# Column sums of squares on TensorE in place of VectorE adds, in the first two norms of a hybrid state-space backbone

## The chip, the cores and the metric

The kernel runs on one core of one Trainium2 chip. The metric is the device time of one execution in microseconds (us). The kernel before took 1124.67 us, the median of three runs (1123.05 to 1126.91).

## The reference

Two trunk layers work on 512 latent tokens of 1024 features, with a prefix of 256 context tokens. What matters here is the beginning of the first layer: a position embedding is added to x, then x and ctx are normalised by the root of the mean square over the features, scaled and shifted by a modulation that comes from `c` (for x) or `c_ctx` (for ctx), and projected.

```python
def rms_norm(x, g):
    xf = x.astype(jnp.float32)
    y = xf * lax.rsqrt(jnp.mean(xf * xf, axis=-1, keepdims=True) + EPS)
    return (y * g.astype(jnp.float32)).astype(x.dtype)
...
h = x + grid_pos_embed(ROWS, x.dtype)[None]
...
n_x = modulate(rms_norm(h, norm_mix_g[i]), sh1, sc1)
n_c = modulate(rms_norm(hc, norm_mix_g[i]), csh1, csc1)
```

Then come state-space groups (a scan over 512 + 256 tokens in 32 groups of 16 channels, with parameters that are discretised in the kernel), a convolution branch, an output projection, a squared-ReLU MLP, a second layer with a pooling mixer and another MLP, and a final norm.

## The kernel before, in words

Activations lie with features on the 128 partitions: x is `x0`, eight tiles `x0[:, d]` of 128 features by 512 tokens, ctx eight tiles of 128 by 256. A norm needs the sum of squares over all 1024 features of each token, that is, over eight tiles and over 128 partitions.

The program is written down as calls, and a planner lays the instructions of each engine in an order: it simulates the program with durations of its own, takes what is ready, and among that what was written first. Each engine then runs its queue strictly in that order, SyncE's queue of DMA issues too. So small work that is written later, such as the discretisation of the state-space parameters (`discretise`, L501, its tile is `scr`), stands between the steps of the norm on VectorE wherever the planner saw room, and a changed duration can move instructions in all queues of the program.

The opening is written in this order (L864 on): `u_load(d)` issues the DMAs of feature tile d (two blocks of modulation weights `wah` and `wraw`, a block of projection weights `wu`); `u_ada(d)` multiplies the modulation vectors with them (L363, 32 narrow matmul records on TensorE), ScalarE copies the result out of PSUM, a selector matmul folds it (L369), and VectorE finishes the tile `ab`. `norm_x` (L385) adds the position to each tile of x on VectorE, squares it on ScalarE, and adds the squares up on VectorE in two accumulators `sx`. `norm_c` (L397) does the same for ctx, two tiles at once, in one accumulator, with no position. Both end in `bcast_rsqrt` (L182): for each block of 128 tokens a matmul with the square as weights and one column of ones (L187) sums over the partitions and gives the tokens' sums as a column of 128 partitions; VectorE scales (`rs_x`, L122), GpSimd raises to the power -1/2 (`rs_y`), VectorE builds a diagonal (`dg`), a matmul with ones spreads it over all partitions (`ps_r`, L194), and ScalarE copies it to `Rs`.

Then `x_step(d)` (L460) scales a tile of x by `Rs` and modulation (`tn`), splits it into two reduced-precision parts (`nh`, `nl`), and multiplies it with the projection weights, twelve 512-wide matmuls into the four banks `ux` (L448 to L450). `c_step(d)` (L464) does it for ctx with six into `uc`; its order among the x steps is `CORD`. The weights are split into two parts by ScalarE and VectorE first (`w_step`, L452). When `discretise` is done, ScalarE writes its power tables `PG` and `PO` (L570). After the last tile, `ux` and `uc` are copied out and transposed (L904), and TensorE goes on with the convolution branch (`vgt`, L760) and the scan.

PSUM is full: bank tag `m` is one bank, used by `ps_ms` and then `ps_r` of each norm, `n` one bank for the modulation. Squares are held in tag `cv`, which has three buffers of 512 elements; two tiles of ctx squares fit one. ScalarE's copies and splits are L139, VectorE's additions L113, subtractions L116 and fused operations L125.

Of the kernel before, what the change touches and what calls it, by code (L numbers as in the profile page):

```python
# [8 lines left out]
F32 = mybir.dt.float32  # L9
F32R = mybir.dt.float32r  # L10
I32 = mybir.dt.int32
AF = mybir.ActivationFunctionType
# [4 lines left out]
D = 1024  # L17
L = 512
LC = 256
KT = 8  # L20
# [77 lines left out]
def body(tc, I, out, dbg=None):  # L98
    nc = tc.nc
    V, S, G, PE = nc.vector, nc.scalar, nc.gpsimd, nc.tensor  # L100
# [5 lines left out]
    def tt(e, o, a, b, op):  # L106
        e.tensor_tensor(o, a, b, op=op)

    def mul(e, o, a, b):
        e.tensor_tensor(o, a, b, op=OP.mult)  # L110

    def add(e, o, a, b):
        e.tensor_tensor(o, a, b, op=OP.add)  # L113
# [4 lines left out]
    def ts(o, a, s1, op0, s2=None, op1=None):  # L118
        if s2 is None:
            V.tensor_scalar(o, a, s1, None, op0=op0)  # L120
        else:
            V.tensor_scalar(o, a, s1, s2, op0=op0, op1=op1)  # L122
# [7 lines left out]
    def E(what, i):  # L130
        t = ENG[what]
        return {"V": V, "G": G, "S": S}[t[i % len(t)]]
# [4 lines left out]
    def copy(e, o, a):  # L137
        if e is S:
            S.activation(o, a, AF.Copy)  # L139
        else:  # L140
            e.tensor_copy(o, a)
# [10 lines left out]
    with tc.tile_pool(name="persist", bufs=1) as P, tc.tile_pool(name="ps", bufs=1, space=PSUM) as PS:  # L152
# [3 lines left out]
        ident = P.tile([128, 128], F32, name="ident")  # L156
        ones = P.tile([128, 128], F32, name="ones")
        mod = P.tile([128, 2, 6, KT], F32, name="mod")

        def smv(n):  # L160
            o, w = SM[n]
            return sm[:, o:o + w]
# [3 lines left out]
        cv = smv("cv").rearrange("p (s j) -> p s j", s=3)  # L166


        def rsqrt_small(ps_ap, m, n, scale):
            x = P.tile([128, 4], F32, name="rs_x", tag="rs_x", bufs=2)[:m, :n]  # L170
            y = P.tile([128, 4], F32, name="rs_y", tag="rs_y", bufs=2)[:m, :n]
            ts(x, ps_ap, scale, OP.mult, EPS, OP.add)
            tt(G, y, x, mhalf[:m, :n], OP.pow)
            return y

        def blocks(ntok):
            nj = -(-ntok // 128)
            while ntok % nj:
                nj += 1
            return nj, ntok // nj  # L180

        def bcast_rsqrt(sums, ntok, dim, tag="m"):  # L182
            nj, m = blocks(ntok)
            ps = bank("ps_ms", tag)
            for j in range(nj):
                for i, sq in enumerate(sums):
                    PE.matmul(ps[:m, j:j + 1], sq[:, j * m:(j + 1) * m], ones[:, 0:1], start=i == 0,  # L187
                              stop=i == len(sums) - 1)
            y = rsqrt_small(ps[:m, :nj], m, nj, 1.0 / dim)
            dg = tmp("dg")[:m, 0:ntok]  # L190
            mul(V, dg.rearrange("p (a b) -> p a b", a=nj), ident[:m, None, :m].to_broadcast([m, nj, m]),
                y[:, :, None].to_broadcast([m, nj, m]))
            pr = bank("ps_r", tag)
            PE.matmul(pr[:, :ntok], ones[:m], dg, start=True, stop=True)  # L194
            return pr[:, :ntok]
# [4 lines left out]
        def bank(nm, tag):  # L200
            return PS.tile([128, 512], F32, name=nm, tag=tag, bufs=dict(s=2, c=2, m=1, n=1)[tag])

        def tmp(nm, n=512, dt=F32):
            return P.tile([128, 512], dt, name=nm, tag="t", bufs=NTMP)[:, :n]

        def htile(nm, shape):
            return P.tile(shape, F32, name=nm, tag="H", bufs=1)
# [44 lines left out]
        def add_pos_k(e, t, d):  # L252
            hv = t[:, d].rearrange("p (k r m) -> p k r m", k=T, r=8)
            if d < 4:
                pe = posr[:, d, None, :, None]
            else:
                pe = posc[:, d - 4].rearrange("p (m k) -> p k m", k=T)[:, :, None, :]
            add(e, hv, hv, pe.to_broadcast([128, T, 8, 8]))
# [46 lines left out]
        def mixer0(P0):  # L305
# [16 lines left out]
            def w4(nm, tag, dt=F32, n=512):  # L322
                w = dict(cv=SLOT, g=1024, r=2 * GQ * NJ).get(tag, 512)
                return P0.tile([128, w], dt, name=nm, tag=tag, bufs=SLOTS[tag])[:, :n]
# [7 lines left out]
            x0 = htile("x0", [128, KT, L])  # L332
            load_x(x0, "xK")
            ctx = P0.tile([128, KT, LC], F32, name="ctx", tag="A")
# [42 lines left out]
            def small(n=NG, dt=F32):  # L377
                r = scr[:, used[0]:used[0] + n]
                used[0] += n
                return r.bitcast(dt) if dt is not F32 else r  # L380

            sx = P0.tile([128, 2, L], F32, name="sx", tag="ysb")
            Rs = [small(L), small(LC)]

            def norm_x():  # L385
                for d in range(KT):
                    add_pos_k(E("pos", d), x0, d)
                    if d < 2:
                        S.activation(sx[:, d], x0[:, d], AF.Square)
                    else:  # L390
                        q = w4("sq", "cv")
                        S.activation(q, x0[:, d], AF.Square)
                        add(V, sx[:, d % 2], sx[:, d % 2], q)
                add(V, sx[:, 0], sx[:, 0], sx[:, 1])
                copy(S, Rs[0], bcast_rsqrt([sx[:, 0]], L, D))

            def norm_c():  # L397
                qs = []
                for d in range(0, KT, 2):
                    q = w4("sq", "cv")  # L400
                    S.activation(q.rearrange("p (a b) -> p a b", a=2), ctx[:, d:d + 2], AF.Square)
                    if qs:
                        add(V, qs[0], qs[0], q)
                    qs.append(q)
                add(V, qs[0][:, 0:LC], qs[0][:, 0:LC], qs[0][:, LC:2 * LC])
                copy(S, Rs[1], bcast_rsqrt([qs[0][:, 0:LC]], LC, D))


            Br_, Bi_ = (P0.tile([128, NG * PH], F32, name="Bx", tag="K2", bufs=2) for _ in range(2))
# [454 lines left out]
            u_load(0)  # L864
            u_ada(0)
            norm_x()
            u_load(1)
            w_step(0)
            x_step(0)
            u_ada(1)  # L870
            norm_c()
            cf = None
            for d in range(1, KT):
# [27 lines left out]
            for i in range(0, NG, 4):  # L901
                ps = bank("ps_u", UT[i // 4])
# [72 lines left out]
        with tc.tile_pool(name="pre", bufs=1) as P0:  # L975
            EPOS = (V, G, V, G, V, G, V, G)
            h, oparts = mixer0(P0)


        with tc.tile_pool(name="main", bufs=1, reuse_waits="tile") as M:  # L980
# [5 lines left out]
            for t, tk in enumerate(HALF):  # L986
                for d in range(KT):
                    ps = tuple(p for p in (1, 0) if (p, t, d) in oparts)
# [156 lines left out]
            for tk in HALF:  # L1145
                n = tk.stop - tk.start
# [122 lines left out]
```

## Time and profile before

| | |
|---|---|
| median of three runs | 1124.67 us |
| profiled execution | 1127.26 us, its span 1125.1 us, around it 2.2 us |
| TensorE busy | 1045.0 us of the span, 7342 matmul records |
| VectorE busy | 810.7 us |
| ScalarE busy | 514.6 us |
| HBM traffic | 158 GB/s over the span |

Times in the rows are microseconds from the span's start, unless marked ns. PE is TensorE's matmul, PEld its weight load (which overlaps it), DVE is VectorE, ACT ScalarE, POOL GpSimd, SP SyncE. L187 is line 187 of the kernel. An fp32 matmul shows as two matmul records. Of several instructions that a row merges (x4), it gives the first start and their busy time together. A matmul's end is modelled, so a row of matmuls lasts somewhat into the next one.

### The profile page before, as it was taken

Reading aid. Unit: us, or ns where it says so; the run is one execution under the profiler, and the core shown is the slowest. Engines: PE = TensorE matmul, PEld = TensorE weight load, DVE = VectorE, ACT = ScalarE, POOL = GpSimd, SP = SyncE. Lnnn points to the kernel's source line nnn. Section 1 sums busy time; section 2 is a strip of 40 time slices with the busy share of each in tenths; the row PEclk is TensorE's granted clock in tenths of the full one; section 3 lists DMA queues with packets and bytes.
Section 4 is the critical chain, followed back from the end, with each engine's and each line's share of the span. In section 5 each row is a group of like instructions: output and inputs, shape, how many; then the busy total and the mean of one; then the engine's idle time right before and its main releaser. Section 6 shows DMA issues by size and latency. Waiting matters only on the chain.

```text
span 1125.1 us, 18913 instructions
## 1 busy us (share of the span) xinstructions
PE 1045.0 (93%) x7342; PEld 892.9 (79%) x7342; DVE 810.7 (72%) x1511; ACT 514.6 (46%) x910; POOL 23.8 (2%) x44
## 2 busy tenths in 40 slices
PE   3879998985998999999999999989989999999996
PEld 2657665544788988888789999989989988888896
DVE  7965699778688989868746679899866553343365
ACT  4365544454755643313325456566545332133253
POOL 0002000000000000000000000000000000000000
PEclk9999899997899999999999999999989999999998
DMA  9430634145546788878745555545535522233252
GB/s 348 146 128 30 184 85 148 44 123 187 160 137 208 208 281 290 304 230 282 242 149 170 182 174 186 162 133 177 160 121 181 178 94 94 95 108 97 94 169 94
DMA packets 63594, 185.09 MB, mean 165 GB/s; under 512 B 8464, under 2 KB 14608, under 8 KB 63376
## 3 DMA queue, kind: packets, MB, share of 16 engines
q1 hardware_dynamic: 63504, 183.87, 50.6%
q8 instruction: 58, 0.95, 0.3%
q14 instruction: 32, 0.26, 0.1%
HBM read 175.22 MB, written 2.10 MB: 158 GB/s over the span
## 4 chain that ended last, share of the span: by engine, by line
PE 53%; DMA 8%; DVE 6%; ACT 1%; issue 1%; POOLq 0%; POOL 0%; DVEq 0%; ACTq 0%
PE ps L150 17%; PE ps L149 17%; PE ps L148 17%; DMA wraw<-in_wadaT 5%; DMA wraw<-in_w 3%; DVE junk L1000 2%; DVE wlo L116 2%; ACT whi L139 1%; PE ps_o L148 0%; PE ps_r L194 0%; DVE tn L125 0%; PE ps_o L150 0%; PE ps_o L149 0%; PE ps_p L150 0%; PE ps_p L148 0%
## 5 line engine op out<-in xcount | busy, mean ns | idle before, releaser
L139 ACT ACTIVATE whi<-wraw 128x1024 fp32r<-128x1024 f32 (+1 forms) x232 | 231.7, 1000 | 397.2 <-PE ps L149 268.9
L116 DVE TENSOR_TENSOR wlo<-wraw,whi 128x1024 fp32r<-128x1024 f32 (+1 forms) x232 | 266.3, 1149 | 107.4 <-ACT whi L139 104.5
L148 PE MATMUL ps<-nh,whi 128*128 128x256 f32 (+3 forms) x768 | 245.8, 322 | 4.4 <-ACT nh L285 2.5
L150 PE MATMUL ps<-nh,wlo 128*128 128x256 f32 (+3 forms) x768 | 246.4, 322 | 1.8 <-DVE wlo L116 1.7
L149 PE MATMUL ps<-nl,whi 128*128 128x256 f32 (+3 forms) x768 | 246.7, 322 | 1.2 <-DVE nl L125 1.2
L148 PE MATMUL ps<-hh,whi 128*128 128x512 f32 (+3 forms) x768 | 244.3, 318 | 0.0
L150 PE MATMUL ps<-hh,wlo 128*128 128x512 f32 (+3 forms) x768 | 243.7, 317 | 0.1
L149 PE MATMUL ps<-hl,whi 128*128 128x512 f32 (+3 forms) x768 | 243.4, 317 | 0.0
L148 PEld LDWEIGHTS ps<-nh,whi 128*128 128x128 f32 x768 | 148.0, 194 | 15.7 <-ACT nh L285 3.7
L150 PEld LDWEIGHTS ps<-nh,wlo 128*128 128x128 f32 x768 | 148.0, 193 | 13.2 <-DVE wlo L116 3.1
L149 PEld LDWEIGHTS ps<-nl,whi 128*128 128x128 f32 x768 | 148.1, 193 | 11.8 <-DVE nl L125 1.7
L150 PEld LDWEIGHTS ps<-hh,wlo 128*128 128x128 f32 x768 | 144.2, 188 | 12.0 <-DVE wlo L116 0.9
L149 PEld LDWEIGHTS ps<-hl,whi 128*128 128x128 f32 x768 | 144.3, 188 | 10.6
L148 PEld LDWEIGHTS ps<-hh,whi 128*128 128x128 f32 x768 | 144.5, 188 | 9.9
L125 DVE SCALAR_TENSOR_TENSOR h<-ps,mod,h 128x512 f32<-128x512 f32 (+3 forms) x96 | 54.9, 571 | 85.9 <-PE ps L150 85.9
L1000 DVE SCALAR_TENSOR_TENSOR junk<-wraw,csil 128x1024 f32<-128x1024 f32 x56 | 68.3, 1220 | 19.9 <-DMA wraw<-in_wadaT 19.6
L116 DVE TENSOR_TENSOR hl<-rl,hh 128x256 fp32r<-128x256 f32 (+3 forms) x96 | 48.5, 511 | 4.8 <-ACT hh L139 3.7
L1026 ACT ACTIVATE rl<-ps 128x256 f32<-128x256 f32 (+3 forms) x96 | 41.9, 437 | 5.7 <-PE ps L150 4.6
L148 PE MATMUL ps_o<-nh,whi 128*128 128x256 f32 x128 | 38.2, 299 | 3.6 <-ACT whi L139 3.0
L150 PE MATMUL ps_o<-nh,wlo 128*128 128x256 f32 x128 | 37.2, 295 | 1.8 <-DVE wlo L116 1.8
L149 PE MATMUL ps_o<-nl,whi 128*128 128x256 f32 x128 | 36.8, 288 | 0.1
L363 PE MATMUL ps_ada<-wraw,S 128*32 128x128 f32 x512 | 25.7, 311 | 9.4 <-DMA wraw<-in_wada0b 8.5
(266 smaller groups left out, 1371.1 us busy)
## 6 DMA issues: line engine op xcount, KB each, us to landing
wraw<-in_w SPq DMA_DIRECT2D x192, 512.0 KB, 3.5
wraw<-in_wadaT SPq DMA_DIRECT2D x56, 512.0 KB, 4.6
wraw<-in_wada0b SPq DMA_DIRECT2D x24, 512.0 KB, 4.4
wraw<-in_wout SPq DMA_DIRECT2D x32, 256.0 KB, 2.6
cvt<-vpad SPq DMA_DIRECT2D x64, 67.5 KB, 2.0
wah<-in_wada SPq DMA_DIRECT2D x16, 256.0 KB, 3.8
wraw<-in_wada SPq DMA_DIRECT2D x8, 512.0 KB, 8.1
wraw<-in_win_vg SPq DMA_DIRECT2D x8, 512.0 KB, 4.2
```

What stands on the lines that cost most here:

```text
L116: e.tensor_tensor(o, a, b, op=OP.subtract)
L125: V.scalar_tensor_tensor(o, a, s, b, op0=op0, op1=op1)
L139: S.activation(o, a, AF.Copy)
L148: PE.matmul(ps, wh, xh, start=first, stop=False)
L149: PE.matmul(ps, wh, xl, start=False, stop=False)
L150: PE.matmul(ps, wl, xh, start=False, stop=last)
L363: PE.matmul(ps[32 * j:32 * j + 32, i * 128:i * 128 + 128], S2[:, kt, :], w[kt], start=kt % 2 == 0, stop=kt % 2 == 1, tile_position=(0, 32 ...
L1000: V.scalar_tensor_tensor(junk, w, 1.0, csil, op0=OP.mult, op1=OP.mult, accum_out=r)
L1026: S.activation(t, ps, AF.Relu)
```

## The change

Both norms go through one new function, `rms`. For each feature tile it takes the square as it comes and lets TensorE sum it over the partitions at once: one column matmul for each block of 128 tokens, accumulated in PSUM over the eight feature tiles. The VectorE additions of squares and the accumulator `sx` are gone; all squares of x go through the three buffers `cv`. What follows the sum (scaling, power, diagonal, broadcast matmul, copy) is the same, and so is the PSUM bank.

```diff
-            sx = P0.tile([128, 2, L], F32, name="sx", tag="ysb")
...
+            def rms(v, n, sqs, tag):
+                nj = n // 128
+                ps = bank("ps_ms", tag)
+                for d in range(KT):
+                    q = sqs(d)
+                    for j in range(nj):
+                        PE.matmul(ps[:, j:j + 1], q[:, 128 * j:128 * j + 128], ones[:, 0:1], start=d == j == 0,
+                                  stop=d == KT - 1 and j == nj - 1)
+                y = rsqrt_small(ps[:, :nj], 128, nj, 1.0 / D)
...
+                copy(S, Rs[v], pr[:, :n])
...
             def norm_x():
-                for d in range(KT):
+                def sq(d):
                     add_pos_k(E("pos", d), x0, d)
-                    if d < 2:
-                        S.activation(sx[:, d], x0[:, d], AF.Square)
-                    else:
-                        q = w4("sq", "cv")
-                        S.activation(q, x0[:, d], AF.Square)
-                        add(V, sx[:, d % 2], sx[:, d % 2], q)
-                add(V, sx[:, 0], sx[:, 0], sx[:, 1])
-                copy(S, Rs[0], bcast_rsqrt([sx[:, 0]], L, D))
+                    q = w4("sq", "cv")
+                    S.activation(q, x0[:, d], AF.Square)
+                    return q
+                rms(0, L, sq, "m")
...
             def norm_c():
                 qs = []
-                for d in range(0, KT, 2):
-                    q = w4("sq", "cv")
-                    S.activation(q.rearrange("p (a b) -> p a b", a=2), ctx[:, d:d + 2], AF.Square)
-                    if qs:
-                        add(V, qs[0], qs[0], q)
-                    qs.append(q)
-                add(V, qs[0][:, 0:LC], qs[0][:, 0:LC], qs[0][:, LC:2 * LC])
-                copy(S, Rs[1], bcast_rsqrt([qs[0][:, 0:LC]], LC, D))
+
+                def sq(d):
+                    if d % 2 == 0:
+                        qs.append(w4("sq", "cv"))
+                        S.activation(qs[-1].rearrange("p (a b) -> p a b", a=2), ctx[:, d:d + 2], AF.Square)
+                    return qs[-1][:, d % 2 * LC:d % 2 * LC + LC]
+                rms(1, LC, sq, "m")
```

## Rows read from the trace of the kernel before

**Rows 1.** The page: TensorE's share, and the chain that ended last.

```profile
PE 1045.0 (93%) x7342; PEld 892.9 (79%) x7342; DVE 810.7 (72%) x1511; ACT 514.6 (46%) x910; POOL 23.8 (2%) x44
...
PE 53%; DMA 8%; DVE 6%; ACT 1%; issue 1%; POOLq 0%; POOL 0%; DVEq 0%; ACTq 0%
```

**Rows 2.** Busy time by stage of 25 us: window and length, engines, clock, DMA share, GB/s.

```profile
0.00:25.00 25.00, 7.44 (x76) 5.46 (x76) 18.63 (x54) 10.37 (x18) 2.71 (x13) 1.00 0.94 341
...
50.00:75.00 25.00, 19.85 (x158) 14.57 (x150) 17.12 (x42) 18.49 (x35) 0.00 (x0) 0.93 0.34 107
...
100.00:125.00 25.00, 22.25 (x209) 16.57 (x207) 3.50 (x7) 12.32 (x30) 0.16 (x2) 0.86 0.43 128
```

**Rows 3.** The opening cut at its events; busy PE, PEld, DVE, ACT, POOL in turn.

```profile
9.70:20.40 10.70, 3.71 (x36) 2.30 (x36) 10.70 (x22) 6.73 (x13) 0.00 (x0) 1.00 1.03 411
20.40:29.30 8.90, 7.43 (x50) 5.69 (x50) 8.65 (x43) 3.62 (x7) 1.66 (x2) 1.00 1.04 406
29.30:36.00 6.70, 6.68 (x28) 4.21 (x28) 6.64 (x30) 2.10 (x5) 0.50 (x1) 1.00 0.18 57
36.00:46.00 10.00, 7.22 (x75) 5.09 (x72) 8.16 (x53) 2.70 (x7) 0.00 (x0) 0.98 0.64 210
...
56.00:69.00 13.00, 7.85 (x63) 5.52 (x61) 8.30 (x20) 12.36 (x26) 0.00 (x0) 1.00 0.23 72
```

**Rows 4.** VectorE's timeline: two adds of x's squares, and the last of ctx.

```profile
17.08 1.28 DVE L113 TENSOR_TENSOR sx<-sx,sq 128x512 f32<-128x512 f32 x2
...
24.81 0.42 DVE L113 TENSOR_TENSOR sq<-sq 128x256 f32<-128x256 f32 x1
```

**Rows 5.** The column sum's line: ns min/median/max, first and last start.

```profile
L187 PE MATMUL ps_ms<-ones,sx x8: 352/352/373, 20.4 to 21.9; 128*128 128x1 f32 x8
```

**Rows 6.** TensorE's timeline in the opening: start, busy us, instruction, count.

```profile
14.63 1.08 PE L363 MATMUL ps_ada<-wraw,S 128*32 128x128 f32 x16
...
20.43 1.87 PE L187 MATMUL ps_ms<-ones,sx 128*128 128x1 f32 x8 [0.85 <-DVE sx L113]
...
27.77 1.01 PE L187 MATMUL ps_ms<-ones,sq 128*128 128x1 f32 x4
29.32 0.80 PE L448 MATMUL ux<-wuhl,nh 128*128 128x512 f32 x1 [0.53 <-ACT nh L285]
29.91 0.63 PE L449 MATMUL ux<-wuhl,nh 128*128 128x512 f32 x1
30.33 0.63 PE L448 MATMUL ux<-wuhl,nh 128*128 128x512 f32 x1
...
37.41 0.39 PE L449 MATMUL ux<-wuhl,nh 128*128 128x512 f32 x1
37.64 0.40 PE L448 MATMUL ux<-wuhl,nh 128*128 128x512 f32 x1
```

**Rows 7.** TensorE's timeline in a later norm: four column records, and the next matmul.

```profile
367.21 0.50 PE L187 MATMUL ps_ms<-ones,sq 128*128 128x1 f32 x4
367.57 0.36 PE L150 MATMUL ps<-nh,wlo 128*128 128x256 f32 x1
```

**Rows 8.** ScalarE's timeline: the first two squares of x, and the last.

```profile
9.10 1.23 ACT L389 ACTIVATE sx<-x 128x512 f32<-128x512 f32 x2 [4.98 <-DVE x L113]
...
17.09 0.63 ACT L392 ACTIVATE sq<-x 128x512 f32<-128x512 f32 x1 [0.92 <-DVE sx L113]
```

**Rows 9.** TensorE's waits, 29 to 130 us: us, times, longest.

```profile
PE uc L448 <- ACT c L285: 5.3, 3, 3.3
```

**Rows 10.** ScalarE's timeline: the first power table, and the weight copy behind the last.

```profile
53.50 2.48 ACT L570 ACTIVATE PG<-scr 64x256 f32<-64x256 f32 x4 [0.93 <-DVE scr L116]
...
65.68 1.15 ACT L139 ACTIVATE wuh<-wu 128x512 fp32r<-128x512 f32 x2
```

**Rows 11.** VectorE's timeline: it reads the sum of x's squares.

```profile
22.51 0.15 DVE L122 TENSOR_SCALAR rs_x<-ps_ms 128x4 f32<-128x4 f32 x1
```

**Rows 12.** VectorE's waits, 9 to 130 us.

```profile
DVE vpad L110 <- PE ps_vg L150: 9.2, 1, 9.2
```

More of the change, by code (lines that the diff above doesn't have):

```diff
@@ L380, in small @@
                 return r.bitcast(dt) if dt is not F32 else r
-            sx = P0.tile([128, 2, L], F32, name="sx", tag="ysb")
             Rs = [small(L), small(LC)]
+            def rms(v, n, sqs, tag):
[7 more added lines that the diff above has]
+                y = rsqrt_small(ps[:, :nj], 128, nj, 1.0 / D)
+                dg = tmp("dg")[:, 0:n]
+                mul(V, dg.rearrange("p (a b) -> p a b", a=nj), ident[:, None, :].to_broadcast([128, nj, 128]),
+                    y[:, :, None].to_broadcast([128, nj, 128]))
+                pr = bank("ps_r", tag)
+                PE.matmul(pr[:, :n], ones, dg, start=True, stop=True)
+                copy(S, Rs[v], pr[:, :n])
```

## The prediction

> **What bounds the kernel now.** I read the page's engines and chain first, then a table by stage, the same table cut at the events of the opening, each engine's timeline there, and last the waits. TensorE (PE) is busy 93% of the span, and the chain that ended last is 53% PE [rows 1]; but that chain is followed back only to 348 us and says nothing of the stretch that is changed. The stage table does: PE works 7.44 of the first 25 us, against 19.85 in 50 to 75 and 22.25 in 100 to 125 [rows 2]. The opening is where PE has room.
>
> Cut more finely [rows 3], VectorE (DVE) is full from 9.7 to 20.4 us (10.70 of 10.70) while PE works 3.71, and all but full to 36 us. DMA is saturated to 29.3 us at about 410 GB/s and nearly idle just after. From 56 to 69 us ScalarE (ACT) is the full one, 12.36 of 13.00. So the limit is first DVE, then PE and DVE together, then ACT, and what leaves or enters one of them has to be followed through the others. PE's queue is in order, and once the projections are done it runs one long branch projection; I assume that a shift there reaches the end unchanged.
>
> **What the change removes.** For x seven DVE adds, for ctx four. In the queue a 128x512 add takes about 0.6 us of DVE (two in 1.28), the last one of ctx 0.4 [rows 4]: 7 x 0.6 = 4.2 and 3 x 0.6 + 0.4 = 2.2, together 6.4 us, in a stretch where DVE is the full engine.
>
> **What it adds.** Before, four column matmuls for x show as 8 records (fp32, two each) [rows 5] and two for ctx as 4 [rows 6]. After, each of eight feature tiles needs four (x) or two (ctx): 64 and 32 records, so 56 and 28 more. The price of one depends on the clock. The eight for x begin between 20.4 and 21.9 us [rows 5], 1.5 / 7 = 0.214 us apart; four in a later stage last from 367.21 until the next matmul at 367.57, 0.09 us each [rows 7]. The granted-clock column reads 1.00 over nearly all of the opening [rows 3], but 512-wide matmuls start 0.42 us apart at 29.91 and 30.33 and 0.23 apart at 37.41 and 37.64 [rows 6], which is about 512 columns at 1.2 and at 2.4 GHz; I go by the spacing and take the low level until about 36 us. In time: x 64 x 0.214 = 13.7 us; ctx 32 x 0.214 = 6.8, or 2.9 at the high level.
>
> **The x norm.** The first of two squares that last 1.23 us together from 9.10 is done at about 9.73 [rows 8]. In front of the last column then lie 13.7 us of columns, the first modulation product (32 records; 16 show 1.08 us [rows 6], so 2.2) and its fold by the selector (four records with as many weight loads as four columns, 0.9). That ends at 26.5 us with PE never idle; before, the sum was there at 20.43 + 1.87 = 22.3 [rows 6]. So +4.2 us. PE's queue is in order and half of that product waits for weights until 14.63 [rows 6]; if all columns stand behind it the end is 14.63 + 1.08 + 13.7 + 0.9 = 30.3, +8.0: the upper bound. If the columns only trail the last square (17.09 + 0.63 = 17.7 [rows 8]) the end comes 3.9 us earlier than before, with eight records behind it at 0.09: the lower bound. I take +4, which goes by the eight records of the same stretch. The steps after it (scaling, power on GpSimd, diagonal, broadcast matmul, copy) are the same in both kernels and move with it.
>
> The squares now go through three buffers that PE frees, so ACT's fourth square waits for PE's first columns, and ACT's copies of the first weights and the first modulation wait behind the squares. They feed the first modulated x, which needs the norm anyway: nothing more on the path. SyncE's queue waits for PE as well, where a buffer of modulation weights comes free, so later loads go out some 4 us later; DMA's busy share falls from 1.04 to 0.18 after 29.3 us [rows 3], so they find it free and overtake nothing. Without that cover they would cost the same 4 us that I already count.
>
> **The ctx norm.** It uses the PSUM bank that x's broadcast leaves, so its columns start only when the x norm has been copied out. Before, its four records stood at 27.77, just ahead of the first projection matmul at 29.32 [rows 6]. If the 32 stand there too, that matmul is 28 x 0.214 = 6.0 us later; behind the rise of the clock they cost 28 x 0.09 = 2.5; if they only fill waits, 0. I take 6.0, as the row puts them there and six of the eight squares fit the three buffers in advance. Queued behind them on PE are the projections of the first two x tiles and the third modulation product, and DVE, which is in order, waits for that one.
>
> **The sum.** PE is 4 + 6 = 10 us late at its first projection. After it, PE has idle to give back: 2.78 us in 36 to 46 and 5.15 in 56 to 69 [rows 3]. The second is a wait for ACT (5.3 us in three waits for the ctx tile `c` [rows 9]), which writes its power tables from 53.50 on, when DVE has delivered their source, until the weight copy at 65.68 [rows 10]. That source comes out of a DVE queue that is 6.4 us lighter, so the tables are hardly later even though DVE waits for PE once; PE's lateness eats the 5.15 us. Of the 2.78, a chain through four engines that mostly moves along, I give it 1. 10 - 5.15 - 1 = about +4 us. The bounds: everything on PE hidden and the whole DVE relief delivered, -6.4; nothing given back, 8.0 + 6.0 = +14. Against the profiled execution's own time, 1127.26 us, the forecast is 1131; that execution is 2.6 above the median of the runs shown, 1124.67, so as a median I write 1129.
>
> **One rule weighed.** From 20.4 to 29.3 us PE was busy 7.43 of 8.90 us [rows 3], with columns, narrow products and two wide matmuls, and still its wide matmuls started 0.42 us apart; only after the wide stream that began at 29.32 did the spacing fall [rows 6]. The Trainium skill ("TensorE: Matmul & The Clock Gate", Part 1: The HAM clock gate) says that the throttle is released by a time of sustained matmul activity and not by a number of matmuls. By it a solid stream of columns from 9.7 us on would bring the high level well before the last of them. The row just told speaks against that for one-column matmuls without settling it, since PE was not solid there for as long as it will be now.
>
> **Rivals.**
> The clock rises during the columns. Then those of x trail the squares: 17.7 + 8 x 0.09 = 18.4 us instead of 22.3, -3.9; ctx +2.5; and 24 matmuls of the first two x tiles start 0.23 instead of 0.42 us apart, -4.6: together -6, 1118.7. It decides if the columns' spacing falls to 0.09 before about 15 us. For it: PE will be solid; against it: the row just told. 0.17.
>
> DVE's relief is worth more than PE's delay. The planner keeps small parameter work on DVE while PE counts columns, the ACT tables start up to 6.4 us before 53.50 [rows 10], and of PE's 10 us its 7.9 of idle take most, so that ACT's chain, not PE's, sets what follows: -6.4 + 2.1 = about -4, 1121. It decides if the tables start before 50 us. For it: DVE is full for 26 us; against it: DVE reads the sum at 22.51 now [rows 11] and must stand still wherever that read comes before PE is done. 0.14.
>
> It is hidden: 7.9 of PE's 10 us fall into its idle and the other 2 into slack of DVE, which works only 3.50 us in 100 to 125 [rows 2]. 1125, no change. 0.18.
>
> The planner's order gets worse. It lays every queue anew from durations of its own; where it takes the columns for short, it puts DVE's read of the sum early, DVE then stands until 26.5 us with parameter work behind it, the tables start some 4 us later too, and PE's 5.15 us stay idle: 10 us with nothing given back, 1135. It decides if DVE idles several us before that read. For it: such places exist, DVE's wait of 9.2 us for PE at the first gate [rows 12] among them; against it: PE's stretch of 1.87 us was met by DVE work that fits it [rows 6, 11]. 0.15.
>
> **How the numbers follow.** The forecast has 0.36, its own range is 1126 to 1134. About 0.3%, 3.4 us, is what can be told from no change. Slower: 0.30 of the forecast's 0.36 and the planner's 0.15, so 0.45. Same: 0.06 of the forecast, the hidden case's 0.18, 0.03 of DVE's relief and 0.01 of the clock, 0.28. Faster: 0.11 and 0.16, 0.27. The range 1119 to 1138 leaves out about half of the clock's case below, and above it what is worse than +13: 2 in 10 at most.
>
> **What would show it.** Right: 64 column records for x from 9.7 to about 26 us, some 0.21 apart; DVE's read of the sum at 26 to 28 us instead of 22.51; the first projection matmul at 36 to 40 instead of 29.32; less PE idle in 56 to 69; the transposes after the projections some 4 us later. Wrong: columns 0.09 apart from 15 us on; the columns of ctx behind projections; power tables well ahead of 53.50; or a difference that first appears after 125 us, which would be order alone.

## The result, and the profile after

The change made the kernel slower: 1140.38 us median (1137.47 to 1142.51) against 1123.86 for the kernel before on the same chip, a ratio of 1.014 with a 95% interval of 1.0118 to 1.0163. The forecast was 1129.0 with a range of 1119 to 1138: the direction came, the size did not. The profiled execution took 1139.9 us, its span is 1138.1, 13.0 more than before. The medians differ by 16.5 us; the profiled execution of the kernel before was itself 3.4 us above its median.

The page of the changed kernel, TensorE's share and the chain's, as in [rows 1]:

```profile
PE 1057.5 (93%) x7426; PEld 907.4 (80%) x7426; DVE 806.5 (71%) x1500; ACT 515.5 (45%) x910; POOL 22.6 (2%) x44
...
PE 51%; DMA 8%; DVE 7%; issue 1%; ACT 1%; POOLq 0%; POOL 0%; DVEq 0%; ACTq 0%
```

The 84 added records are there (7426 - 7342), and the page says no more. The opening, cut as in [rows 3] (window, length, then busy PE, PEld, DVE, ACT, POOL, the granted clock, DMA):

```profile
9.70:20.40 10.70, 10.34 (x69) 9.43 (x69) 10.22 (x33) 4.59 (x9) 0.00 (x0) 1.00 1.03 412
20.40:29.30 8.90, 8.76 (x64) 8.20 (x64) 4.57 (x26) 5.15 (x10) 1.02 (x1) 1.00 0.85 328
29.30:36.00 6.70, 6.00 (x35) 4.51 (x35) 6.64 (x37) 2.91 (x7) 0.00 (x0) 0.91 0.55 196
36.00:46.00 10.00, 7.48 (x51) 6.16 (x49) 9.82 (x54) 3.00 (x6) 0.82 (x1) 0.67 0.28 84
46.00:56.00 10.00, 4.27 (x11) 3.07 (x12) 3.91 (x12) 8.35 (x18) 0.00 (x0) 0.50 0.13 50
56.00:69.00 13.00, 11.95 (x100) 8.36 (x98) 8.16 (x15) 3.52 (x9) 0.00 (x0) 0.90 0.26 81
```

TensorE is solid to 29.3 us, as forecast, and full in 56 to 69, where it had idled. But between 46 and 56 us it works 4.27 of 10.00 us while ScalarE works 8.35: a hole that the kernel before does not have there:

```profile
46.00:56.00 10.00, 10.00 (x62) 7.42 (x63) 10.00 (x32) 4.33 (x9) 0.00 (x0) 0.85 0.34 110
```

Three engines show how it comes about. TensorE's timeline in the changed kernel (start, busy us, instruction, count, idle before):

```profile
10.06 6.96 PE L390 MATMUL ps_ms<-ones,sq 128*128 128x1 f32 x32 [10.06 <-ACT sq L404]
...
20.31 4.43 PE L390 MATMUL ps_ms<-ones,sq 128*128 128x1 f32 x20
24.60 0.99 PE L369 MATMUL ps_ada<-sel,ada 128*128 128x2 f32 x4
...
29.48 2.04 PE L397 MATMUL ps_r<-dg,ones 128*128 128x512 f32 x2 [0.31 <-DVE scr L125]
...
32.38 3.12 PE L390 MATMUL ps_ms<-ones,sq 128*128 128x1 f32 x24 [0.52 <-ACT scr L139]
...
35.99 0.80 PE L458 MATMUL ux<-wuhl,nh 128*128 128x512 f32 x1
...
42.70 0.70 PE L363 MATMUL ps_ada<-wraw,S 128*32 128x128 f32 x14
45.93 1.19 PE L397 MATMUL ps_r<-dg,ones 128*128 128x256 f32 x2 [2.52 <-DVE dg L110]
52.85 1.01 PE L369 MATMUL ps_ada<-sel,ada 128*128 128x2 f32 x4 [5.73 <-ACT ada L139]
53.72 0.77 PE L458 MATMUL ux<-wuhl,nh 128*128 128x512 f32 x1
```

In the kernel before, the second x tile's first projection and the fold of the third modulation, and on ScalarE that modulation's copy:

```profile
37.07 0.50 PE L448 MATMUL ux<-wuhl,nh 128*128 128x512 f32 x1
41.21 0.61 PE L369 MATMUL ps_ada<-sel,ada 128*128 128x2 f32 x4 [0.54 <-ACT ada L139]
...
40.77 0.38 ACT L139 ACTIVATE ada<-ps_ada 128x256 f32<-128x256 f32 x1 [3.03 <-PE ps_ada L363]
```

ScalarE's timeline in the changed kernel: the power tables, then the copy of the third modulation and the split of the second x tile:

```profile
42.97 2.38 ACT L580 ACTIVATE PG<-scr 64x256 f32<-64x256 f32 x4 [8.38 <-DVE scr L116]
...
50.08 2.31 ACT L580 ACTIVATE PO<-scr 64x256 f32<-64x256 f32 x4
52.41 0.38 ACT L139 ACTIVATE ada<-ps_ada 128x256 f32<-128x256 f32 x1
52.82 0.72 ACT L285 ACTIVATE nh<-tn,ab 128x512 fp32r<-128x512 f32 x1
```

VectorE's: a split of weights, the sum of x, the sum of ctx, ctx's diagonal, and the second x tile right behind it:

```profile
24.30 0.69 DVE L116 TENSOR_TENSOR wuhl<-wu,wuhl 128x512 fp32r<-128x512 f32 x1 [3.87 <-ACT wuhl L139]
...
27.34 0.16 DVE L122 TENSOR_SCALAR rs_x<-ps_ms 128x4 f32<-128x4 f32 x1 [0.23 <-PE ps_ms L390]
...
44.28 0.14 DVE L122 TENSOR_SCALAR rs_x<-ps_ms 128x2 f32<-128x2 f32 x1
45.36 0.42 DVE L110 TENSOR_TENSOR dg<-ident,rs_y 128x256 f32<-128x256 f32 x1
45.70 0.74 DVE L125 SCALAR_TENSOR_TENSOR tn<-x,ab,scr 128x512 f32<-128x512 f32 x1
```

The third modulation's product ends at 43.4 us, and its copy stands behind 9.4 us of tables that began at 42.97 instead of 53.50 [rows 10]. VectorE's lost adds are only part of that: summed from its timelines, its work on x and ctx tiles (`tn`, `nl`, `c`) in front of the tables fell from 7.9 to 1.5 us: those tiles were late, and the parameter work now stands ahead of them. The second x tile's `tn`, which shares a ring of buffers with `dg`, is written at 45.70 behind ctx's diagonal, and its split too stands behind the tables. So the second x tile's projections begin at 53.72 instead of 37.07 us.

A small account of each kernel's opening is used from here on, summed from TensorE's timeline of its profile: where the first projection starts, how long TensorE idles from there to the end of the last projection of x, and what is left, its work. Before: 29.32 + 12.1 + 55.5 = 96.9. After: 35.99 + 16.3 + 56.9 = 109.2. That is 12.3 us, and the span grew by 13.0: what is lost at 109 us is still lost at the end.

### The profile page after: what moved, and what is told of

The parts are those of the page before. It is cut to its first block, busy times and chain, and to the rows that moved or that the text cites. A ratio compares the mean times of both kernels' runs of the same rounds, so it can differ in the third digit from the quotient of the medians.

```text
span 1138.1 us, 19072 instructions
## 1 busy us (share of the span) xinstructions
PE 1057.5 (93%) x7426; PEld 907.4 (80%) x7426; DVE 806.5 (71%) x1500; ACT 515.5 (45%) x910; POOL 22.6 (2%) x44
## 4 chain that ended last, share of the span: by engine, by line
PE 51%; DMA 8%; DVE 7%; issue 1%; ACT 1%; POOLq 0%; POOL 0%; DVEq 0%; ACTq 0%
PE ps L150 16%; PE ps L149 16%; PE ps L148 16%; DMA wraw<-in_wadaT 6%; DVE junk L1010 2%; DVE wlo L116 2%; DMA wraw<-in_w 2%; ACT whi L139 1%; DVE tn L125 1%; PE ps_o L148 0%; PE ps_r L194 0%; PE ps_o L150 0%; PE ps_o L149 0%; PE ps_p L150 0%; PE ps_p L148 0%
## 5 line engine op out<-in xcount | busy, mean ns | idle before, releaser
L149 PEld LDWEIGHTS ps<-nl,whi 128*128 128x128 f32 x768 | 147.6, 192 | 11.5 <-DVE nl L125 1.4
L266 ACT ACTIVATE sq<-h 128x256 f32<-128x256 f32 (+2 forms) x64 | 24.8, 408 | 16.6 <-DVE h L125 15.0
```

The costliest lines, as they stand in the source:

```text
L149: PE.matmul(ps, wh, xl, start=False, stop=False)
L266: S.activation(q, h[:, d, tk], AF.Square)
```

## The experiments

Each run has its median in us and, in that order, its ratio to the kernel before on the same chip and the 95% interval of the ratio. The code shown is shortened to the lines that matter. One profile's opening is not sharper than about 4 us: columns for x alone, profiled twice, ended its last projection at 89.1 and at 93.2 us.

**One half of the change at a time.** `x_only` keeps ctx's adds, `c_only` keeps x's.

```diff
 x_only                                   c_only
+    rms(0, L, sq, "m")       # norm_x    +    rms(1, LC, sq, "m")      # norm_c
     (norm_c as before)                        (norm_x as before)
```

> Only the x norm sums by columns; the ctx norm keeps its VectorE adds. Theory P (TensorE's columns themselves, mostly the 64 of x, are the loss): most of the changed kernel's +16 us stays, about 1134 to 1138. Theory C (the late sum of ctx, read at 44.28 instead of 28.82 us, holds the second x tile, and ScalarE's tables slip in front of it): ctx's sum is early again, x's sum still at about 27 us; what stays is the 4.8 us of the x sum less what waits give back, 1126 to 1130.

> Only the ctx norm sums by columns; the x norm keeps its VectorE adds. Theory P: only 28 records more on TensorE, 2 to 6 us, partly hidden: 1124 to 1129. Theory C: x's sum is read at 22.5 as before, but ctx's comes some 10 us later than 28.8, and the second x tile with it: 1128 to 1133, most of the changed kernel's loss after its 4.8 us are taken off.

Columns for x alone: 1116.27, 0.9942 (0.992 to 0.9964), faster; again in five rounds 1119.53, 0.9945 (0.9922 to 0.9967). The ratio is as expected there; the time is 1.5 us above, on a chip where the kernel before took 1126.39:

> Columns for x alone once more, in five rounds: if the gain stands, 1114 to 1118, 0.4 to 0.8% under the kernel before.

Columns for ctx alone: 1124.57, 1.0016 (0.9998 to 1.0034), no change. Theories P and C both expected `x_only` to lose and miss it; for `c_only` P's time came and C's did not, although ctx's sum was late there too (read at 37.82 us). So neither half loses anything and the two together lose 16 us: no theory that prices the parts and adds them can hold, mine included. In the first profile of x's columns the first projection is 4.9 us late, about as forecast for x's norm, but the account reads 34.22 + 8.1 + 46.8 = 89.1:

```profile
30.60 1.08 PE L363 MATMUL ps_ada<-wah,S 128*32 128x128 f32 x16
31.46 1.08 PE L363 MATMUL ps_ada<-wraw,S 128*32 128x128 f32 x16
...
34.22 0.50 PE L459 MATMUL ux<-wuhl,nh 128*128 128x512 f32 x1 [0.52 <-ACT nh L285]
34.56 0.40 PE L460 MATMUL ux<-wuhl,nh 128*128 128x512 f32 x1
34.80 0.39 PE L459 MATMUL ux<-wuhl,nh 128*128 128x512 f32 x1
```

The third modulation's product stands in front of the first projection, while x's norm is copied out and the first tile is scaled and split, and the projections start about 0.23 us apart, where they started 0.42 apart before [rows 6]. The second profile has the same order, but its projections start at 36.67 and 0.42 apart, and the gain in time stands (0.9945): it does not hang on that spacing.

**The tables later, and the diagonal in its own tile.** Both in the changed kernel:

```diff
 after_late
+    with tc.issue_after(nhi[-1]):        # behind the split of the third x tile
         rows(...)                        # the sixteen table writes
 after_dg
-    dg = tmp("dg")[:, 0:n]
+    dg = tmp("dg")[:, 0:n] if v == 0 else P0.tile(..., name="dgc", tag="ysb")[:, 0, 0:n]
```

> The changed kernel with ScalarE's sixteen power-table writes queued behind the third x tile's split (an issue-order edge only, nothing else is written differently). Theory T (tables as one block of 9.4 us in front of the third modulation's copy and of the second x tile's split are the loss): both come at 44 to 47 us instead of 52.4 and 52.8, and 5 to 9 us of the total come back, 1131 to 1135. Theories P and C without T: the tables only fill a wait, 1138 to 1141.

> The changed kernel with a tile of its own for the diagonal of the ctx norm, so that the second x tile's scaled copy no longer takes its buffer after it. Theory C: the second x tile starts at about 35 us instead of 45.7, before the tables; TensorE works through it from 42 on: 4 to 8 us come back, 1132 to 1136. Theory P: no change, 1138 to 1141. Theory T: TensorE still waits for the third modulation's copy until 52 us behind the tables, so at most 3 us come back.

> The changed kernel with both repairs: ctx's diagonal in a tile of its own (the second x tile no longer waits behind it) and ACT's power tables queued behind the third x tile. Alone the repairs gave 1131.8 and 1133.4 us, 8.6 and 7.0 below the changed kernel's 1140.4. Theory A (two separate losses, each with its own mechanism): they add up, 1140.4 - 8.6 - 7.0 = about 1125, no slower than the kernel before by more than 0.3%, and PE has no idle of several us between 40 and 60 us. Theory S (one loss, the late third modulation, which either repair frees by itself or which both only shift): together no better than the better one alone, 1130 to 1133, with PE still idle some 5 us ahead of the third modulation's fold.

`after_late`: 1133.4, 1.009 (1.0064 to 1.0116). `after_dg`: 1131.82, 1.0068 (1.0043 to 1.0093). Both together, `after_dg_late`: 1141.96, 1.0163 (1.011 to 1.0215). Each alone gives 7 to 8 us back, together nothing: they do not add, theory A falls, and S's time (1130 to 1133) misses too. Each alone, TensorE still waits once for the fold of a modulation whose copy stands behind the tables; with the tables late, and with the diagonal apart:

```profile
58.53 0.73 PE L370 MATMUL ps_ada<-sel,ada 128*128 128x2 f32 x4 [4.88 <-ACT ada L139]
```

```profile
53.43 1.01 PE L369 MATMUL ps_ada<-sel,ada 128*128 128x2 f32 x4 [5.00 <-ACT ada L139]
```

With both it is the same wait once more (4.87 us), and the first projection is later still: 38.01 + 11.8 + 58.5 = 108.3. The wait moves from one modulation to the next. TensorE's idle from the first projection on is 11.5 to 11.8 us in all three, no more than before (12.1), and still they lose: their first projections are 7.3 to 8.7 us late. Why the two repairs together are worse than either is open.

**No tables at all**, in both kernels (the branch is then not the reference's):

```diff
-    rows(o, kb if o is PG else kf, 0, sg)
-    rows(o, kf if o is PG else kb, 64, sg)
+    G.memset(o, 0.5)
```

> The kernel before with ScalarE's sixteen writes of the power tables left out (the two tables are filled with a constant by GpSimd, so the branch is not the reference's); run together with the changed kernel cut in the same way. TensorE's wait of 5.15 us in 56 to 69 us goes. Theory T (the tables in ScalarE's queue are what turned the change's lateness into a loss): about 5 us below before, 1118 to 1120, and the changed kernel without tables comes within 7 to 10 us of it, where with tables it is 16.3 slower. Theory N (the tables are not the cause, the loss is the lay of the queues as a whole): the difference between the two stays 13 to 18.

> The changed kernel with the sixteen writes of the power tables left out in the same way. Theory T: it gains more than the kernel before does, because the block stands in front of both the third modulation and the second x tile here: 1140.4 - 7 (what queueing them later gave) - 5 (the wait that was left then) = 1126 to 1130, 7 to 10 us over the kernel before without tables. Theory N: 1132 to 1137, 13 to 18 over it.

`before_notab`: 1115.77, 0.9918 (0.989 to 0.9945). `after_notab`: 1132.52, 1.006 (1.0028 to 1.0092). Both gain about 8 us, the difference stays 16.7: theory N. The tables cost each kernel a wait, but are not what sets the two apart. Here TensorE idles alike from the first projection on (7.0 and 7.6 us) and the last projection is 9.5 us later, 7.1 of it already at the first one (36.34 against 29.24). The spans differ by 15.0; the other 5.5 arise behind 97 us, and I did not trace them.

**The columns of ctx behind the third modulation.** In the changed kernel and its repairs 24 of ctx's columns stand in front of the first projection and of that product. In `c_only` they do too, and it loses nothing:

```profile
25.88 5.28 PE L403 MATMUL ps_ms<-ones,sq 128*128 128x1 f32 x24
31.02 0.77 PE L463 MATMUL ux<-wuhl,nh 128*128 128x512 f32 x1
...
38.69 0.61 PE L369 MATMUL ps_ada<-sel,ada 128*128 128x2 f32 x4 [0.56 <-ACT ada L139]
```

There x's sum is early (read at 21.01 us), and the third modulation is folded at 38.69, ahead of the tables (45.18). So the columns' place can cost only together with x's later sum. The next three runs keep both halves and move ctx's columns. `after_written` only writes ctx's norm later, which changes the order in which the buffers are handed out; `after_modfirst` also queues it behind the fold; `after_mod_dg` is that with the diagonal apart.

```diff
-    norm_c()                             # behind u_ada(1)
 ...
     u_ada(d)
+    if d == 2:
+        with tc.issue_after(adas[2].last.ins):     # after_written: without this line
+            norm_c()
```

> The changed kernel with ctx's norm written behind the third modulation and, on TensorE, queued behind its fold (all 32 columns of ctx then stand behind the first six projections). Theory Q (the loss of both together is the 24 columns of ctx in front of the first projection and the third modulation): first projection at 32 to 33 us instead of 35.99, 1119 to 1126, about the kernel before. Theory L (the loss is that ctx's sum comes late and the second x tile's diagonal buffer and the tables follow it, wherever the columns stand): ctx's sum is read as late as or later than at 44.28, 1133 to 1141.

> The same, and ctx's diagonal in a tile of its own, so that the second x tile does not wait for ctx's sum. Theory Q: as the kernel with the moved columns alone, 1119 to 1126. Theory L: it frees the second x tile and gains over that kernel, 1122 to 1130.

> The changed kernel with ctx's norm only written behind the third modulation, not queued behind it: 24 of ctx's 32 columns stay in front of the first projection, but the second x tile gets its buffer before ctx's diagonal. Theory Q (the columns in front of the first projection and the third modulation are the loss): most of it stays, 1130 to 1140, first projection at 36 to 38 us. Theory B (the buffer order, which the written order decides): the loss goes as far as with both edits, 1123 to 1128.

`after_modfirst`: 1125.26, 0.9994 (0.9975 to 1.0014). `after_mod_dg`: 1127.71, 1.0016 (0.9995 to 1.0038). `after_written`: 1136.51, 1.0112 (1.0067 to 1.0156). The same 64 + 32 columns, and the whole loss is gone with their place; with the written order alone most of it stays. Theory Q holds for kernels that have x's columns (1127.71 is a little above its range). The edge on the queue lets the planner lay the other queues anew too, so more than the columns moved. TensorE's timeline of `after_modfirst`:

```profile
31.57 1.08 PE L363 MATMUL ps_ada<-wah,S 128*32 128x128 f32 x16 [1.28 <-DVE ab L113]
...
33.44 0.80 PE L458 MATMUL ux<-wuhl,nh 128*128 128x512 f32 x1
...
36.87 2.70 PE L390 MATMUL ps_ms<-ones,sq 128*128 128x1 f32 x12
...
45.88 2.29 PE L390 MATMUL ps_ms<-ones,sq 128*128 128x1 f32 x20
...
52.74 0.61 PE L369 MATMUL ps_ada<-sel,ada 128*128 128x2 f32 x4 [2.15 <-ACT ada L139]
```

and of `after_written`:

```profile
31.33 5.28 PE L390 MATMUL ps_ms<-ones,sq 128*128 128x1 f32 x24 [0.21 <-ACT scr L139]
...
37.11 0.80 PE L458 MATMUL ux<-wuhl,nh 128*128 128x512 f32 x1
...
53.29 1.01 PE L369 MATMUL ps_ada<-sel,ada 128*128 128x2 f32 x4 [2.66 <-ACT ada L139]
```

In `after_modfirst` the tables still run from 42.64 to 52.30 us and a modulation's copy still stands behind them. But it is the fourth one: the third is folded at 36.16, between the projections, so both first x tiles are projected by 45.9, and 20 columns, which nobody needs before, run under the tables. Account: 33.44 + 8.9 + 54.2 = 96.5, which gives back all of the change's 12.3 us. Ctx's sum is read at 48.20 us, later than in the changed kernel, so lateness of that sum is by itself no cost: theory L falls.

One time sorts all the kernels: when the third modulation is folded on TensorE. Before, that is 41.21 us. It comes later in every kernel that is slower (44.56 to 53.43; without tables 43.54 against 39.95) and earlier in every kernel that is not (33.10 to 38.69). It does not price them: 50.93 in `after_dg_late` goes with 1.0163, 53.43 in `after_dg` with 1.0068.

**Where the gain of x's columns comes from.** `x_relief` leaves x's adds out and adds no columns (the norm is then not the reference's); `x_only_adds` has the columns and keeps the adds as dead work; `x_only_dg` has ctx's diagonal apart.

```diff
 x_relief                                  x_only_adds
-    add(V, sx[:, d % 2], sx[:, d % 2], q)      rms(0, L, sq, "m")
-    add(V, sx[:, 0], sx[:, 0], sx[:, 1])  +    add(V, sx[:, d % 2], sx[:, d % 2], q)   # read by nobody
```

> The kernel before with x's seven adds left out and no columns in their place (the last square alone stands for the sum, so the norm is not the reference's; ctx unchanged). It asks where the 7.3 us come from that columns for x alone gave (1116.3 against 1123.6). Theory R (VectorE's relief of 4.2 us in its full stretch): as fast or faster than that, 1110 to 1117, because nothing is added on PE. Theory O (the gain is the order of the queues that the later x sum brought: the third modulation ahead of the projections and a denser stream of projections): no gain, 1121 to 1126.

> Columns for x only, with x's adds kept on VectorE as dead work into a tile that nobody reads (ctx by adds as before). Theory R (relief): the gain of the columns for x alone goes; PE's 56 columns are then a pure cost, 1124 to 1130 (x sum some 5 us later, no relief). Theory O (order): the gain stays, 1115 to 1119. If PE's columns cost nothing at all and the relief is all of the gain: 1122 to 1125.

> Columns for x only, and ctx's diagonal in a tile of its own. With columns for x alone the second x tile's product is written at 36.80 us, right behind ctx's diagonal at 36.47, but the modulation it needs is there only a little before that. The theory that the buffer order costs by the time that ctx's sum is late (C) expects little here, since nothing is late: 1113 to 1117, at most 3 us below columns for x alone (1116.3). If the buffer order were a cost of its own at every place: as much as in the changed kernel, 1108 to 1110.

`x_relief`: 1123.56, 0.9988 (0.9961 to 1.0015). `x_only_adds`: 1123.35, 0.9998 (0.9973 to 1.0024). `x_only_dg`: 1118.99, 0.9945 (0.9916 to 0.9974). The relief without the columns gains nothing that can be measured, nor do the columns without the relief. Theory O fits the first and misses the second, theory R the other way round: the gain came only with the two together, and what it rests on is not shown. The diagonal's place adds nothing, as expected where ctx's sum is not late.

**Wide matmuls in place of the columns**, for x:

```diff
-    for j in range(nj): PE.matmul(ps[:, j:j + 1], q[...], ones[:, 0:1], ...)
+    PE.matmul(pq[:, :n], ident, q, start=d == 0, stop=d == KT - 1)     # then a copy, four columns
```

> x's squares summed over the feature tiles on TensorE by 512-wide matmuls with the identity (16 records) instead of 64 one-column ones, then four columns of the sum as in the kernel before; ctx by adds. It asks whether wide matmuls raise TensorE's clock where columns did not, and what the relief of VectorE is worth with less work on TensorE. In the changed kernel the columns ran 0.21 us apart from 10 to 27 us and the clock did not rise. Theory W (the clock follows what TensorE does, and wide matmuls are what raises it): the wide matmuls, 0.42 apart at first, come 0.23 apart before the first projection, which starts at the high level some 4 us earlier than in the kernel before: 1114 to 1119. Theory M (any busy TensorE counts the same, and the changed kernel's low level has another reason): they stay 0.42 apart throughout, first projection at 27 to 30 at the low level: 1120 to 1126.

`x_wide`: 1121.3, 0.9982 (0.9956 to 1.0008): no gain that can be measured. TensorE's timeline answers half of each theory:

```profile
15.65 0.64 PE L363 MATMUL ps_ada<-wah,S 128*32 128x128 f32 x16
16.23 1.13 PE L389 MATMUL ps_ms<-sq,ident 128*128 128x512 f32 x2
...
21.43 1.05 PE L187 MATMUL ps_ms<-ones,sm 128*128 128x1 f32 x8 [0.39 <-ACT sm L139]
22.41 0.64 PE L363 MATMUL ps_ada<-wah,S 128*32 128x128 f32 x16
...
27.70 1.01 PE L187 MATMUL ps_ms<-ones,sq 128*128 128x1 f32 x4
```

After eight wide records the narrow product takes 0.57 us (15.65 to 16.23; at the low level 0.86, 30.60 to 31.46 above), and the columns at 21.43 are 0.12 apart: the level rose. By 27.70 they are 0.23 apart again, and the first projections run 0.42 apart from 31.10 to 31.95 us, then 0.23. Its last projection ends at 89.5, 7.4 us earlier than before, and yet the span of that execution (1125.5, the slowest of its ten) is no shorter: what is won in the opening does not always reach the end.

**The tables in three portions**, with columns for x alone, behind the splits of the fourth, fifth and sixth x tiles:

```diff
+    for i in {3: (0, 1), 4: (2,), 5: (3,)}.get(d, ()):
+        with tc.issue_after(nhi[-1]):
+            rows(*todo[i])               # one of four groups of four writes
```

> Columns for x only, with the power tables written in three portions behind the splits of the fourth (two of the four groups), fifth and sixth x tiles instead of 16 writes in two near blocks. With columns for x alone TensorE still waits 5.12 us until 62.5 us for a split of ctx that stands behind the tables. Theory T: that wait goes or shrinks to under 2 us: 1111 to 1114, the fastest of all. Theory N: another wait of the same size takes its place, since ScalarE has to do the same work before VectorE can use the tables: 1115 to 1119.

> Columns for x alone with the tables in three portions, in five rounds on the same chip as columns for x alone: its last projection ended 4 us earlier in the profile (85.06 against 89.12 us), its time was not lower. If what is won before 89 us reaches the end: 2 to 4 us below columns for x alone. If a later limit takes it back: the same within 2 us.

`x_only_spread`: 1117.0, 0.9929 (0.9897 to 0.9961), and in five rounds 1114.67, 0.9908 (0.9877 to 0.9939). The wait for ctx behind the tables is gone, as theory T had it; the longest left up to the last projection is 2.1 us. The first time lies in theory N's range, the second 4.9 us below columns for x alone. It is the fastest version tried and beats both kernels; over columns for x alone (0.9942 and 0.9945) its lead lies inside the intervals.

## Why the prediction was wrong

**The x norm: right.** 64 records from 10.06 to 27.3 us, 0.21 apart (20 in 20.31 to 24.60), the sum read at 27.34 against 22.51 [rows 11]: +4.8, forecast +4. That this alone costs time is not borne out: with x alone the kernel was faster.

**The ctx norm: placed right, sized too high, its followers not priced.** 24 columns stand in front of the first projection, which starts at 35.99, +6.7 where the sum had +10. Of that, x's sum is 4.8, so ctx's columns cost about 2 where I took 6.0: the 24 ran 0.13 us apart, not 0.214 (3.12 us for all). I named what is queued behind them, two x tiles and the third modulation, and counted for it only the delay of the columns. That the third modulation would be folded at 52.85 instead of 41.21 us is in no term.

**The sum: the step that failed.** "That source comes out of a DVE queue that is 6.4 us lighter, so the tables are hardly later even though DVE waits for PE once; PE's lateness eats the 5.15 us." The tables were not late: they came 10.5 us early, 42.97 against 53.50, and the modulation's copy, at 40.77 before, came late, so that the two crossed on ScalarE's in-order queue. From the first projection on TensorE's idle went from 12.1 to 16.3 us where I had it fall by 6.15. The 5.15 us in 56 to 69 were indeed eaten, but two new waits, 2.52 and 5.73 us, stood between 43.4 and 52.85. So of the 12.3 us the first projection has 6.7, the idle 4.2, the work 1.4, where I had 10, -6.15 and nothing. By `after_modfirst` against `after_written`, with x's columns there, the place of ctx's columns and of the third modulation decides, not the number of columns or ctx's lateness; by `c_only` that place costs nothing where x's sum is early; by the kernels without tables the crossing with the tables is not the only way to lose. How the late modulation turns into so many us when there are no tables stays open.

**What follows the opening: right.** 12.3 us at the last projection, 13.0 in the span. It is no rule: see `x_wide`.

**The rivals.** VectorE's relief had its condition met (tables before 50 us) with the sign turned: the early tables stood in front of what TensorE needed. The planner's order getting worse is the nearest in its class and in its time (1135), but not as I had put it: VectorE did idle 3.87 us ahead of x's sum, up to 24.30, but for ScalarE's copy of weights and not for that sum (0.23 us); the tables were early all the same, and TensorE's long wait was for ScalarE. The clock did not rise in x's columns, as I held.

## What to carry to other kernels

Work that goes into an in-order queue is to be judged by what stands behind it there, one instruction at a time: ask which engine gets its operand late, and what becomes ready earlier on that engine and slips in front. Price parts of a change together, not one by one: here two halves, one at -7 us and one at 0, made +16. If a change relieves one engine and loads another, put the new work where the loaded engine waits anyway.

## What the hardware showed that I had not expected

One-column matmuls did not raise TensorE's level here and did not always hold it. In the changed kernel they ran 0.21 us apart, the low level by the spacing, while TensorE was busy 10.34 of 10.70 and 8.76 of 8.90 us; the granted-clock column reads 1.00 there, as it does in [rows 3]. Behind the two wide records at 29.48 the 24 ctx columns ran 0.13 apart, and the first projections behind those were 0.42 apart again, the low level (1.2 GHz), to 41.7 us. Neither is regular: in `after_written` the 24 in the same place took 5.28 us, 0.22 apart, and in `after_modfirst` 20 columns ran 0.11 apart from 45.88 us and the product behind them, from 48.09, was still at the high level (16 records in 0.46 us). The Trainium skill ("TensorE: Matmul & The Clock Gate", Part 1: The HAM clock gate) speaks of sustained matmul activity; taken for one-column matmuls, this trace does not agree with it: the level stayed low through the columns and narrow products from 10.06 to 27.3 us, and in the kernel with wide sums it was high behind eight 512-wide records. Why columns differ, no run here tells.
